# Windowed attention in a mixer block: two tiles per step, the far key as a diagonal, and a reordered first stage

## The chip, the cores and the metric

The kernel runs on one core of a Trainium2 chip. The metric is the device time of one execution in microseconds (us); the median of three runs is 2248.58 us, from 2247.2 to 2249.55.

## What is computed

A decoder block on 2048 rows of 1024 channels, in float32. A conditioning vector gives shift, scale and gate (`c @ w_ada + b_ada`); h is the RMS-normed x, scaled and shifted. One input projection of h gives queries, keys and values of 24 heads in three groups, and the inputs of a pooling mixer and of the gates. A query attends 129 keys of its group, itself and 128 back, in steps of 1, 4 or 16 rows; the third group is done on subsequences of step 8, where the bias leaves every second key out:

```python
def dilated_window_attention(q, k, v, dil, n_back, bias_g):
    dist = BLOCK + i - j
    band_ok = (dist >= 0) & (dist <= n_back)
    logits = jnp.einsum('znqhd,znkhd->znhqk', qb, kb).astype(jnp.float32) * (HEAD_DIM ** -0.5)
    logits = jnp.where(mask[None, :, None], logits + bias[None, None], -jnp.inf)
    p = jnp.exp(logits - m)
    o = jnp.einsum('znhqk,znkhd->znqhd', p.astype(vb.dtype), vb).astype(jnp.float32)
```

The three groups of a head slot are combined with softmax weights of their log denominators, gated, and projected; the pooling branch likewise; the sum goes through `w_out`, the gate, the residual and a final RMS norm.

## The kernel before, in words

The rows are done in two halves of 1024 (`h`). Float32 products are made of three: every operand is split into a high and a low part (`whi`, `wlo`; `hhi`, `hlo`; `khi`, `klo`), and high by high, high by low and low by high are added up. Weights come as 176 raw blocks of 128 x 1024 (`fetch_raw`, line 203, two buffers), and each half block is split by a cast on DVE (`whi`, line 216) and a subtraction on POOL (`wlo`, line 217), as `fetch_part` is called from `tick`.

**First stage** (`first_unit`). x is normed and transposed into `xT`; the conditioning weights come in four blocks of 256 columns (`ada_load`); DVE sums each over 8 chunks (`ada_sum`, lines 377 and 379), PE adds up over partitions (`ada_columns`, line 388), DVE makes scale and shift (lines 391 to 394), ACT makes two chunks of h per block (`h_chunk`, lines 398 and 400) and DVE or POOL their low part (line 401). The k, q and v products of the first unit (line 466) take a chunk as it comes. At its end come the bias tables (`bias_tables`, line 320), built in DRAM from `fd`, and the bias of the first unit (`load_bias`, line 528).

**Units and attention.** A unit is 128 columns of q, k and v of one group: two heads (24 units over both halves). Its main products (`mm3`, line 252) are woven with the attention of the unit before it: `weave` spreads the attention's steps over the 24 steps of the main products. The order on PE and SP, DVE, ACT and POOL is the order in which the code is run through. An attention has 8 tiles of 128 queries. Step s makes the logits of tile s (line 619: for each of the two heads three products of a 64-row operand, in one PSUM bank per head), adds bias and takes the maximum (line 622), the exponentials (line 626); two steps later the current-key logits are transposed (`transposed`, line 650) and `pT` is made twice, once masked for the previous block's values (line 658) and once plain (line 659); a step later come the outputs (`output`, line 669) with `v` and with `vd`, previous minus current values (line 656). The key at distance 128 shares its place with the one at distance 0, so its weight is taken out by a dot product with the identity (line 637, after the add of line 635) and added to the output with `vd` (line 676). Group 0, whose steps are 13 instead of 11, joins the three groups (lines 693 to 708) and transposes the result (`joined`, line 712).

**Second half's h.** While the last products (`out_half`, line 932, column blocks of 256; `yt`, line 946, and the squares on ACT, line 912) of the first half run, `next_h` loads x in pairs of tiles (`new_x`, line 273), norms them (`x_norm`, lines 290, 277 and 292) and transposes (line 336) them chunk by chunk into the new h. Large tiles share `NBIG` = 34 buffers of 128 x 1024, handed out in the order of the code; a load waits until the tile that had the buffer has been read.

## Time and profile before

| | |
|---|---|
| median of three runs | 2248.58 us (2247.2 to 2249.55) |
| the profiled execution, its own time | 2248.75 us |
| its span in the profile | 2246.9 us |
| mean granted clock of TensorE | 0.986 |
| PE busy | 2165.3 us, 11786 products |
| DVE, ACT, POOL busy | 1026.7, 601.8, 762.5 us |

The span is the time from the first to the last instruction in the profile; the execution's own time has 1.85 us more around it. A line of PE rows gives a product of the 128 x 128 array; x2 is two of them in a row, and the time beside it is from the start of the first to the end of the last, so that the distance to the next row's start is what they cost where they follow closely.

### The profile page before, as it was taken

To read this page: it belongs to the slowest core of one execution; us is meant where nothing else is said; L and a number is where in the kernel's file an instruction comes from. 1 tells how busy PE (TensorE), PEld (TensorE's weight loads), DVE (VectorE), ACT (ScalarE), POOL (GpSimd) and SP (SyncE) were. 2 spreads that over 40 slices of the span, in tenths; PEclk is the share of its full clock that TensorE was granted. 3 is DMA by queue.
4 is the path that set the end of the run, shared out by engine and by line. 5 is a ranking of instruction groups with operands and counts; after the bars stand their busy time and mean duration, and the time that the engine had idled before them with its cause. 6 is when DMAs were issued, how large, how long until landed. Compare 5 with 4: busy or idle time off the path is not lost.

```text
span 2246.9 us, 32404 instructions
## 1 busy us (share of the span) xinstructions
PE 2165.3 (96%) x11786; PEld 1810.7 (81%) x11786; DVE 1026.7 (46%) x3188; ACT 601.8 (27%) x1554; POOL 762.5 (34%) x682
## 2 busy tenths in 40 slices
PE   3799999999999999999899999999999999999998
PEld 2588888888887888888888888888888788888898
DVE  5545526355284111115764475664744931111164
ACT  4333323333232001002433333333333320010023
POOL 3322212112134224446752222222222342253375
PEclk7999999999999999999999999999999999999999
DMA  7343312223211112114432322223233111121144
GB/s 275 101 147 105 88 58 83 80 79 88 63 60 47 47 53 88 48 47 160 160 119 74 113 79 88 77 88 93 72 95 91 56 41 53 38 94 47 48 132 160
DMA packets 142687, 198.58 MB, mean 88 GB/s; under 512 B 13542, under 2 KB 109983, under 8 KB 142528
## 3 DMA queue, kind: packets, MB, share of 16 engines
q1 hardware_dynamic: 142528, 196.51, 27.4%
q8 instruction: 94, 1.54, 0.3%
q14 instruction: 65, 0.53, 0.1%
HBM read 157.62 MB, written 35.16 MB: 86 GB/s over the span
## 4 chain that ended last, share of the span: by engine, by line
PE 85%; POOL 4%; DVE 4%; DMA 3%; issue 3%; SPq 1%; ACT 0%; POOLq 0%; DVEq 0%; ACTq 0%
PE mm L252 68%; PE knot L669 6%; PE qk L619 4%; PE mm L932 2%; PE knot L650 2%; POOL wlo L217 2%; DMA wraw<-in_wpk_dram 1%; PE knot L584 1%; DMA wada<-in_w_ada_dram 1%; POOL y L911 1%; PE hp L855 0%; DVE whi L216 0%; PE mm L466 0%; POOL hlo L401 0%; SPq L320 0%
## 5 line engine op out<-in xcount | busy, mean ns | idle before, releaser
L217 POOL TENSOR_TENSOR wlo<-wraw,whi 128x512 fp32r<-128x512 f32 x352 | 468.0, 1333 | 990.3 <-DVE whi L216 536.3
L252 PE MATMUL mm<-hhi,whi 128*128 128x512 f32 x2000 | 649.1, 406 | 2.0 <-DVE klo L508 2.0
L252 PE MATMUL mm<-hlo,whi 128*128 128x512 f32 x2000 | 621.8, 392 | 0.0
L252 PE MATMUL mm<-hhi,wlo 128*128 128x512 f32 x2000 | 619.2, 391 | 0.0
L216 DVE CAST whi<-wraw 128x512 fp32r<-128x512 f32 x352 | 191.8, 549 | 693.3 <-PE mm L252 515.3
L252 PEld LDWEIGHTS mm<-hlo,whi 128*128 128x128 f32 x2000 | 376.7, 188 | 83.2
L252 PEld LDWEIGHTS mm<-hhi,wlo 128*128 128x128 f32 x2000 | 376.3, 188 | 82.9
L252 PEld LDWEIGHTS mm<-hhi,whi 128*128 128x128 f32 x2000 | 355.2, 189 | 79.1 <-issue 2.9
L626 ACT ACTIVATE l<-l,row 128x256 f32<-128x256 f32 (+1 forms) x384 | 181.4, 473 | 253.0 <-DVE row L622 246.4
L749 ACT ACTIVATE sg<-mm 128x1024 f32<-128x1024 f32 x48 | 49.4, 1028 | 554.8 <-PE mm L252 422.5
L622 DVE CUSTOM_DVE_ANT_0 l<-qk,bias 128x256 f32<-128x256 f32 (+1 forms) x384 | 132.8, 383 | 92.0 <-PE qk L619 66.1
L659 ACT COPY pT<-knot 128x256 f32<-128x256 f32 x192 | 71.7, 373 | 329.0 <-DVE pT L658 234.4
L932 PE MATMUL mm<-whi,mhi 128*128 128x256 f32 x512 | 149.8, 293 | 6.0 <-DVE yt L946 3.5
L932 PE MATMUL mm<-whi,mlo 128*128 128x256 f32 x512 | 146.9, 287 | 2.7 <-POOL mlo L756 2.7
L932 PE MATMUL mm<-wlo,mhi 128*128 128x256 f32 x512 | 146.6, 286 | 0.0
L669 PE MATMUL knot<-v,pT 128*128 128x64 f32 x768 | 130.0, 262 | 1.3 <-ACT pT L659 1.3
L656 POOL TENSOR_TENSOR vd<-v 128x128 f32<-128x128 f32 x88 | 52.6, 601 | 224.4 <-DVE row L676 144.7
L669 PEld LDWEIGHTS knot<-v,pT 128*128 128x128 f32 x768 | 113.6, 191 | 4.1 <-ACT pT L659 2.3
L669 PE MATMUL knot<-vd,pT 128*128 128x64 f32 x560 | 108.3, 275 | 0.0
L658 DVE TENSOR_TENSOR pT<-knot,prevm 128x256 f32<-128x256 f32 x140 | 58.9, 420 | 103.1 <-PE knot L669 99.6
L932 PEld LDWEIGHTS mm<-whi,mhi 128*128 128x128 f32 x512 | 100.1, 195 | 6.9 <-DVE yt L946 3.7
L932 PEld LDWEIGHTS mm<-whi,mlo 128*128 128x128 f32 x512 | 99.9, 195 | 3.5 <-POOL mlo L756 3.5
(168 smaller groups left out, 2627.0 us busy)
## 6 DMA issues: line engine op xcount, KB each, us to landing
wraw<-in_wpk_dram SPq DMA_DIRECT2D x176, 512.0 KB, 3.7
rows<-row SPq DMA_DIRECT2D x128, 66.0 KB, 1.6
row<-rows SPq DMA_DIRECT2D x64, 132.0 KB, 3.5
x<-in_x_dram SPq DMA_DIRECT2D x16, 512.0 KB, 4.8
wada<-in_w_ada_dram SPq DMA_DIRECT2D x32, 256.0 KB, 5.5
y<-in_x_dram SPq DMA_DIRECT2D x16, 512.0 KB, 7.5
out_dram<-yo SPq DMA_DIRECT2D x16, 512.0 KB, 6.5
khist<-kh SPq DMA_DIRECT2D x52, 128.0 KB, 2.6
```

Of the source, the lines that this page charges most:

```text
L216: copy(out=hi, in_=raw)
L217: nc.gpsimd.tensor_tensor(out=lo, in0=raw, in1=hi.bitcast(F32), op=ALU.subtract)
L252: nc.tensor.matmul(ps[:, n * 512:(n + 1) * 512], lhsT=w, rhs=m[:, n * 512:(n + 1) * 512], start=(k == 0 and j == 0), stop=(k == nk - 1 and ...
L619: nc.tensor.matmul(qks[i][:, :nk], lhsT=qt[qi][a], rhs=keys[ki][a], start=(j == 0), stop=(j == 2))
L622: nc.vector.tensor_tensor_reduce(out=l[:, i, :nk], in0=qks[i][:, :nk], in1=bt[:, i, 256 - nk:], scale=-1.0, scalar=1e38, op0=ALU.add, op1= ...
L626: nc.scalar.activation(out=l[:, i, :nk], in_=l[:, i, :nk], func=AF.Exp, scale=-1.0, bias=nm[:, i:i + 1], accum_out=rw[:, 130 + i:131 + i])
L656: nc.gpsimd.tensor_tensor(out=vd, in0=d["prev"], in1=vcur[t], op=ALU.subtract)
L658: nc.vector.tensor_tensor(out=pT[:, 0], in0=pps, in1=m, op=ALU.mult)
L659: nc.scalar.copy(out=pT[:, 1], in_=pps)
L669: nc.tensor.matmul(ops[:, hs], lhsT=d["pT"][:, b, i, :], rhs=vv[:, hs], start=(b == 1), stop=(b == 0 or not full))
L749: nc.scalar.activation(out=s, in_=ps, func=AF.Sigmoid)
L932: nc.tensor.matmul(pst[:, pos:pos + 256], lhsT=st, rhs=mv, start=(fresh and i == 0), stop=(last and i == 2))
```

## The change

- **Pairs.** An attention has 4 pair steps instead of 8 tile steps: 7 steps in place of 11, and 8 in place of 13. A step makes the logits of two tiles, 12 products in a run, into one bank per head (the tiles' halves side by side), four transposes into one bank, and the outputs of both tiles, 16 products at most. The tiles `l` (2 buffers instead of 3, of twice the size), `pT` (1 instead of 2) and `vd` (1 instead of 2) hold a pair.
- **Far key.** POOL multiplies the previous-key part of the exponentials by the identity in place; DVE adds that diagonal to the masked `pT`. The dot products (line 637) and the scaled adds (line 676) go. The output copies (line 679) go from DVE to ACT.
- **First stage.** All three raw blocks are asked for at once, the third in a large tile; the even parts are cast ahead of the first scale, the odd ones on ACT behind the first chunk of h; the sums of a block are made in one go; `hlo` of all chunks but the first and the last on POOL; the products of a chunk go by kind (high by high for k, q and v, and so on). The first group's bias table and the bias are asked for right behind the first scale.
- **Buffers.** 33 large tiles instead of 34; small scratch tiles (`junk`, `hraw`, `fs`, the last `yt`) use the buffers of `khist`.

The core of the diff:

```diff
-NBIG = 34
+NBIG = 33
...
-            t = wp.tile([P, HALF], F32, name="wraw", tag="wraw", bufs=2)
+            t = b4(name="wraw") if i == 2 else wp.tile([P, HALF], F32, name="wraw", tag="wraw", bufs=2)
...
-    def fetch_part(copy=nc.vector.tensor_copy):
-
-        i = state["part"]
+    def fetch_part(i=None, copy=nc.vector.tensor_copy):
+
+        if i is None:
+            i = state["part"]
...
-        state["part"] += 1
+        state["part"] = max(state["part"], i + 1)
         if q == 1:
             del raws[b]
+        if q == 1 and b != 2:
             fetch_raw()
...
-        junk = att.tile([P, D], mybir.dt.bfloat16, name="junk", tag="l", bufs=3)
+        junk = att.tile([P, D], mybir.dt.bfloat16, name="junk", tag="khist", bufs=3)
...
-    def bias_tables():
-
-        for g in GORDER:
+    def bias_tables(gs):
+
+        for g in gs:
...
+        accs = [t[:, i * 512:(i + 1) * 512] for t in (b4(name="ada"), b4(name="ada")) for i in range(2)]
         blocks = [ada_load(0)]
-        fetch_raw()
-        fetch_raw()
+        for _ in range(3):
+            fetch_raw()
         for b in range(1, 4):
             blocks.append(ada_load(b))
-        accs = [b4(name="ada")[:, :512] for _ in range(4)]
...
-        ada_columns(0, accs[0])
-        for _ in range(6):
-            fetch_part()
-        ada_sum(blocks[1], accs[1], range(2))
-        wts = [take("col") for _ in range(3)]
+        ps = ada_columns(0, accs[0])
+        for i in (0, 2, 4):
+            fetch_part(i)
+        ada_scale(0, ps)
+        bias_tables(GORDER[:1])
+        load_bias(g, 0, res)
+        wts = [halves(i, P) for i in (0, 2, 4)]
+        state["used"] += 3
         kp, qp = mm(), mm()
         vp = [ps_qk.tile([P, 512], F32, name="vp", tag="qk") for _ in range(2)]
         dsts = [[kp[:, :512], kp[:, 512:]], [qp[:, :512], qp[:, 512:]], vp]
 
-        def products(k, bs):
+        def products(k, js):
             hhi, hlo = hparts[k]
-            for b in bs:
-                whi, wlo = wts[b][k]
-                for j, (w, m) in enumerate(((whi, hhi), (whi, hlo), (wlo, hhi))):
+            for j in js:
+                for b in range(3):
+                    w, m = (wts[b][k][j == 1], hlo if j == 2 else hhi)
                     for n in range(2):
                         nc.tensor.matmul(dsts[b][n], lhsT=w, rhs=m[:, n * 512:(n + 1) * 512],
                                          start=(k == 0 and j == 0), stop=(k == KC - 1 and j == 2))
 
 
         for b in range(4):
-            h_chunk(2 * b, nc.gpsimd if 0 < b < 3 else nc.vector)
+            h_chunk(2 * b, nc.vector if b == 0 else nc.gpsimd)
+            if b == 0:
+                for i in (1, 3, 5):
+                    fetch_part(i, nc.scalar.copy)
+                for w, q in zip(wts, (1, 3, 5)):
+                    w += halves(q, P)
+            h_chunk(2 * b + 1, nc.gpsimd if b < 3 else nc.vector)
             if b < 3:
-                ada_sum(blocks[b + 1], accs[b + 1], range(4 if b else 2, 8))
-            if b < 2:
-                ada_sum(blocks[b + 2], accs[b + 2], range(4))
-            h_chunk(2 * b + 1, nc.gpsimd if b < 3 else nc.vector)
-            if 0 < b < 3:
-                ada_columns(b + 1, accs[b + 1])
-            products(2 * b, range(2))
-            if b == 0:
-                ada_columns(b + 1, accs[b + 1])
-            products(2 * b, range(2, 3))
+                ada_sum(blocks[b + 1], accs[b + 1], range(8))
+            products(2 * b, range(3))
+            if b < 3:
+                ada_scale(b + 1, ada_columns(b + 1, accs[b + 1]))
...
-        bias_tables()
+        bias_tables(GORDER[1:])
...
-        load_bias(g, 0, res)
...
+        def differences(p):
+
+            d = st[p]
+            if d["prev"]:
+                vd = d["vd"] = att.tile([P, 2, P], F32, name="vd", tag="vd", bufs=1)
+                for a, b, prev in d["prev"]:
+                    nc.gpsimd.tensor_tensor(out=vd.rearrange("p j c -> p (j c)")[:, a * P:b * P], in0=prev,
+                                            in1=v[:, (2 * p + a) * P:(2 * p + b) * P], op=ALU.subtract)
+
...
+            l = att.tile([P, 4, 256], F32, name="l", tag="l", bufs=2)
+            d["l"] = l
+            nks = [size(2 * p), size(2 * p + 1)]
+
+            qks = [ps_qk.tile([P, 512], F32, name="qk", tag="qk") for _ in range(2)]
+            for j, nk in enumerate(nks):
+                t = 2 * p + j
+                k0 = kslot(g, t)
+                if nk == P:
+                    keys = [k[:, k0:k0 + P] for k in ks]
+                elif not edge(t):
+                    keys = [k[:, k0 - P:k0 + P] for k in ks]
+                else:
+                    keys = [kh_t[t][:, i, :] for i in range(2)]
+                qt = [q[:, k0:k0 + P] for q in qs]
+                for n, (qi, ki) in enumerate(((0, 0), (1, 0), (0, 1))):
+                    for i in range(2):
+                        a = slice(64 * i, 64 * i + 64)
+                        nc.tensor.matmul(qks[i][:, j * 256:j * 256 + nk], lhsT=qt[qi][a], rhs=keys[ki][a],
+                                         start=(n == 0), stop=(n == 2))
...
+            prev, cur = l[:, f:, 0:P], l[:, f:, P:256]
+            if g < 2:
+                nc.vector.tensor_tensor(out=cur, in0=cur, in1=prev, op=ALU.add)
+                nc.gpsimd.tensor_tensor(out=prev, in0=prev, in1=ident.unsqueeze(1).broadcast_to([P, 4 - f, P]),
+                                        op=ALU.mult)
...
+        def transposed(p, bank):
+
+
+
+
+            d = st[p]
+            f, l = d["from"], d["l"]
+            for n in range(4):
+                nc.tensor.transpose(bank[:, n * P:(n + 1) * P], l[:, n, P:256], ident)
+            yield
+            pps = bank.rearrange("p (n q) -> p n q", q=P)
+            pT = d["pT"] = att.tile([P, 2, 4, P], F32, name="pT", tag="pT", bufs=1)
+            if f < 4:
+                m = prevm[:, g // 2, :].unsqueeze(1).broadcast_to([P, 4 - f, P])
+                nc.vector.tensor_tensor(out=pT[:, 0, f:], in0=pps[:, f:], in1=m, op=ALU.mult)
                 if g < 2:
-                    d["far"] = sm.tile([P, 2], F32, name="far")
-                    junk = att.tile([P, P], mybir.dt.bfloat16, name="dot", tag="dot", bufs=1)
-                    nc.vector.tensor_tensor(out=cur, in0=cur, in1=prev, op=ALU.add)
-                    for i in range(2):
-                        nc.vector.tensor_tensor_reduce(out=junk, in0=prev[:, i, :], in1=ident, scale=1.0, scalar=0.0,
-                                                       op0=ALU.mult, op1=ALU.add, accum_out=d["far"][:, i:i + 1])
-                else:
-                    for i in range(2):
-                        nc.vector.tensor_tensor(out=cur[:, :, i::2], in0=cur[:, :, i::2], in1=prev[:, :, 1 - i::2],
-                                                op=ALU.add)
-
-        def transposed(t, bank):
-
-            d = st[t]
-            nk = d["nk"]
-            pps = bank[:, :256].rearrange("p (i q) -> p i q", i=2)
-            for i in range(2):
-                nc.tensor.transpose(pps[:, i, :], d["l"][:, i, nk - P:nk], ident)
-            yield
-
-            pT = d["pT"] = att.tile([P, 2, 2, P], F32, name="pT", tag="pT", bufs=2)
-            if nk == 256:
-                vd = d["vd"] = att.tile([P, P], F32, name="vd", tag="vd", bufs=2)
-                nc.gpsimd.tensor_tensor(out=vd, in0=d["prev"], in1=vcur[t], op=ALU.subtract)
-                m = prevm[:, g // 2, :].unsqueeze(1).broadcast_to([P, 2, P])
-                nc.vector.tensor_tensor(out=pT[:, 0], in0=pps, in1=m, op=ALU.mult)
+
+                    nc.vector.tensor_tensor(out=pT[:, 0, f:], in0=pT[:, 0, f:], in1=l[:, f:, 0:P], op=ALU.add)
...
+        for s in range(7 if g else 8):
+            parts_ = []
...
+                if s < 7:
                     parts_.append(output(s - 3, bank))
-                if g == 0 and 5 <= s:
-                    parts_.append(joined(s - 5, bank))
-                for p in parts_:
-                    next(p)
-                if s < 8:
-                    logits(s)
-                for p in parts_:
-                    next(p, None)
-            else:
+                if g == 0 and 4 <= s:
+                    parts_.append(joined(s - 4, bank))
+            for p in parts_:
+                next(p)
+            for p in parts_:
+                next(p, None)
+            if 2 <= s < 6:
+                differences(s - 2)
+                if g == 0:
+                    load_rows(s - 2)
+            if s < 4:
                 logits(s)
+                prefetch(2 * s + 2)
+                prefetch(2 * s + 3)
+            if s < 2:
                 flip(s)
+            if 1 <= s < 5:
+                prefetch_v(s - 1)
...
-                    t = att.tile([P, 256], F32, name="yt", tag="pT", bufs=2)
+                    t = att.tile([P, 256], F32, name="yt", tag="khist", bufs=3)
...
-                n_queue = 11 if g else 13
+                n_queue = 7 if g else 8
```

PE, an attention step of group 1 in the first half (`qk` logits, `knot` the bank of transposes and outputs, `mm` the main products). Before:

```order
L650 MATMUL knot<-ident,l 128x128 x2
L669 MATMUL knot<-v_734,pT 128x64
L669 MATMUL knot<-vd,pT 128x64
L669 MATMUL knot<-v_734,pT 128x64
L669 MATMUL knot<-vd,pT 128x64
L619 MATMUL qk<-khi_715,qhi_719 128x256 x2
L619 MATMUL qk<-khi_715,qlo_720 128x256 x2
L619 MATMUL qk<-klo_716,qhi_719 128x256 x2
L252 MATMUL mm<-hhi_516,whi 128x512 x2
```

and a step of the change that has logits, of group 0:

```order
L684 MATMUL knot<-ident,l 128x128 x4
L705 MATMUL knot<-v_4004,pT 128x64 x3
L705 MATMUL knot<-vd,pT 128x64
L705 MATMUL knot<-v_4004,pT 128x64
L705 MATMUL knot<-vd,pT 128x64
L649 MATMUL qk<-khi_3750,qhi_3899 128x256 x2
L649 MATMUL qk<-khi_3750,qlo_3900 128x256 x2
L649 MATMUL qk<-klo_3751,qhi_3899 128x256 x2
L649 MATMUL qk<-khi_3750,qhi_3899 128x256 x2
L649 MATMUL qk<-khi_3750,qlo_3900 128x256 x2
L649 MATMUL qk<-klo_3751,qhi_3899 128x256 x2
L255 MATMUL mm<-hhi_580,whi 128x512 x2
```

The logits of two tiles now stand in one run, and between two steps of the change lie nine pairs of main products where six lay before.

SP, the queue of the loads, at the end of the first stage (`fd` and `btab` the bias tables, `wraw` raw blocks, `cw` and `pm` constants). Before:

```order
L314 DMA fd<-fs_340 8x383
L314 DMA fd<-fs_345 8x383
L314 DMA fd<-fs_350 8x383
L203 DMA wraw<-in_wpk_dram 128x1024 x6
L320 DMA btab<-fd 1024x1x256 x3
L491 DMA cw<-in_cntw_dram 128x64
L528 DMA bias<-btab 128x2x256
```

and in the change:

```order
L317 DMA fd<-fs 8x383 x3
L323 DMA btab<-fd 1024x1x256
L536 DMA bias<-btab 128x2x256
L203 DMA wraw<-in_wpk_dram 128x1024 x5
L323 DMA btab<-fd 1024x1x256 x2
L500 DMA cw<-in_cntw_dram 128x64
```

The bias moved ahead of five raw blocks, with one table in front of it; the sixth raw block (the third of all) went up to the first two.

SP again, the loads of x for the second half, with what each waits for. Before:

```order
L273 DMA x276_9644<-in_x_dram 128x1024 [waits DMAHW5_49,DMAHW0_49]
L273 DMA x277_9646<-in_x_dram 128x1024 [waits DMAHW1_49,DVE_49,Activation_49]
L203 DMA wraw_9713<-in_wpk_dram 128x1024 [waits DMAHW6_49,Pool_49]
L203 DMA wraw_9826<-in_wpk_dram 128x1024 [waits DMAHW7_49,DMAHW3_49,Pool_49]
L273 DMA x279_9847<-in_x_dram 128x1024 [waits DMAHW4_49,PE_49]
L273 DMA x280_9849<-in_x_dram 128x1024 [waits DVE_49,Activation_49]
```

and in the change:

```order
L276 DMA x272_8846<-in_x_dram 128x1024 [waits DMAHW0_49,DVE_49,Activation_49]
L276 DMA x273_8848<-in_x_dram 128x1024 [waits DMAHW1_49,PE_49]
L203 DMA wraw_8915<-in_wpk_dram 128x1024 [waits DMAHW6_49,Pool_49]
L203 DMA wraw_9028<-in_wpk_dram 128x1024 [waits DMAHW7_49,DMAHW3_49,Pool_49]
L276 DMA x275_9049<-in_x_dram 128x1024 [waits DMAHW4_49,DVE_49,Activation_49]
L276 DMA x276_9051<-in_x_dram 128x1024 [waits DMAHW5_49,PE_49]
```

The second tile of each pair now waits for PE (`PE_49`): its buffer was that of a tile of x whose last transposes stand just ahead of the pass that needs the new one.

## Rows read from the trace of the kernel before

**Rows 1.** The page: busy time, and PE's busy tenths in 40 slices.

```profile
PE 2165.3 (96%) x11786; PEld 1810.7 (81%) x11786; DVE 1026.7 (46%) x3188; ACT 601.8 (27%) x1554; POOL 762.5 (34%) x682
...
PE   3799999999999999999899999999999999999998
```

**Rows 2.** Waits of PE: engine, line, waited for; us in total, times, longest.

```profile
PE mm L466 <- DVE hlo L401: 17.4, 1, 17.4
PE qk L619 <- DVE row L622: 12.8, 1, 12.8
...
PE hp L336 <- DVE x L292: 5.6, 4, 3.2
...
PE mm L932 <- DVE yt L946: 3.5, 1, 3.5
```

**Rows 3.** Timeline, first stage: start, length, engine, line; idle before and its releaser.

```profile
27.25 0.15 DVE L394 TENSOR_TENSOR shift_c<-knot,col 128x2 f32<-128x2 f32 x1
...
41.36 0.76 DVE L216 CAST whi<-wraw 128x512 fp32r<-128x512 f32 x2 [10.47 <-DMA wraw<-in_wpk_dram]
...
52.99 0.48 DVE L377 TENSOR_SCALAR ada<-wada,col 128x512 f32<-128x512 f32 x1
...
56.01 0.15 DVE L394 TENSOR_TENSOR shift_c<-knot,col 128x2 f32<-128x2 f32 x1
...
58.61 5.36 POOL L401 TENSOR_TENSOR hlo<-xT,hhi 128x1024 fp32r<-128x1024 f32 x2 [11.22 <-ACT hhi L400]
...
59.10 2.61 DVE L377 TENSOR_SCALAR ada<-wada,col 128x512 f32<-128x512 f32 x1
...
66.27 0.15 DVE L394 TENSOR_TENSOR shift_c<-knot,col 128x2 f32<-128x2 f32 x1
...
71.69 4.40 DVE L216 CAST whi<-wraw 128x512 fp32r<-128x512 f32 x3
...
89.87 0.70 PE L252 MATMUL mm<-hhi,whi 128*128 128x512 f32 x2 [1.99 <-DVE klo L508]
```

**Rows 4.** Timeline, the first logits after the first stage.

```profile
111.81 0.29 DVE L622 CUSTOM_DVE_ANT_0 l<-qk,bias 128x128 f32<-128x128 f32 x1 [16.14 <-DMA bias<-btab]
```

**Rows 5.** Timeline of PE, one attention step between main products.

```profile
279.90 0.39 PE L669 MATMUL knot<-v,pT 128*128 128x64 f32 x2
280.12 0.39 PE L669 MATMUL knot<-vd,pT 128*128 128x64 f32 x2
280.44 0.38 PE L619 MATMUL qk<-khi,qhi 64*128 64x256 f32 x2
280.66 0.28 PE L619 MATMUL qk<-khi,qlo 64*128 64x256 f32 x2
280.78 0.28 PE L619 MATMUL qk<-klo,qhi 64*128 64x256 f32 x2
280.99 0.73 PE L252 MATMUL mm<-hhi,whi 128*128 128x512 f32 x2
281.56 0.63 PE L252 MATMUL mm<-hlo,whi 128*128 128x512 f32 x2
282.03 0.62 PE L252 MATMUL mm<-hhi,wlo 128*128 128x512 f32 x2
```

**Rows 6.** Groups by line: count | busy, mean ns of one | idle before.

```profile
L217 POOL TENSOR_TENSOR wlo<-wraw,whi 128x512 fp32r<-128x512 f32 x352 | 468.0, 1333 | 990.3 <-DVE whi L216 536.3 <-PE mm L252 331.6 <-PE knot L712 37.3
...
L635 DVE TENSOR_TENSOR l<-l 128x256 f32<-128x256 f32 x108 | 60.9, 564 | 10.0 <-ACT l L626 10.0
```

**Rows 7.** Second half's x: timeline, and the page's DMA issues (us to landing last).

```profile
1114.87 0.38 PE L336 MATMUL knot<-ident,x 128*128 128x128 f32 x2
...
1116.86 1.06 ACT L290 ACTIVATE junk<-x 128x1024 bf16<-128x1024 f32 x1 [0.48 <-POOL hlo L344]
...
1121.27 0.48 PE L336 MATMUL hp<-ident,x 128*128 128x128 f32 x1 [0.94 <-DVE x L292]
...
x<-in_x_dram SPq DMA_DIRECT2D x16, 512.0 KB, 4.8
```

More of the change, by code (lines that the diff above doesn't have):

```diff
@@ L550, in attention @@
         edge = lambda t: g == 2 or (g == 1 and t < 4) or (g == 0 and t == 0)
-        st = [{} for _ in range(8)]
+        size = lambda t: P if h == 0 and edge(t) else 256
+        kh_t = {}
+        st = [{} for _ in range(4)]
         if g == 0:
@@ new lines, in prefetch_v @@
+        def prefetch_v(p):
+            d = st[p]
+            d["prev"] = []
+            t = 2 * p
+            ends = [edge(t), edge(t + 1)]
+            if h == 1 and ends[0]:
+                n = sum(ends)
+                vt = att.tile([P, 2, P], F32, name="vhist", tag="vhist", bufs=2)
+                for j in range(n):
+                    ht = {0: 0, 1: (t + j) % 4, 2: t + j}[g]
+                    nc.sync.dma_start(out=vt[:, j, :], in_=vh[g][hp][ht])
+                d["prev"].append((0, n, vt.rearrange("p j c -> p (j c)")[:, :n * P]))
+            a = sum(ends)
+            if a < 2:
+                t0 = t + a - (1, 4)[g]
+                d["prev"].append((a, 2, v[:, t0 * P:(t0 + 2 - a) * P]))
@@ new lines, in differences, with load_rows @@
+        def differences(p):
[5 more added lines that the diff above has]
+                                            in1=v[:, (2 * p + a) * P:(2 * p + b) * P], op=ALU.subtract)
+        def load_rows(p):
+            r3 = st[p]["row3"] = sm.tile([P, 2, 3, RW], F32, name="row3", tag="row3", bufs=3)
+            for j in range(2):
+                t = 2 * p + j
+                nc.sync.dma_start(out=r3[:, j, 0:2, :], in_=rows[h][hp][t * P:(t + 1) * P])
@@ L661, in output @@
[L661 to L673 removed]
+                    nc.vector.tensor_tensor(out=cur[:, :, i::2], in0=cur[:, :, i::2], in1=prev[:, :, 1 - i::2],
+                                            op=ALU.add)
@@ L674, in output @@
+        def output(p, bank):
+            d = st[p]
+            ops = bank[:, :256].rearrange("p (j c) -> p j c", c=P)
+            for j in range(2):
+                full = 2 * j >= d["from"]
+                vs = [(1, vcur[2 * p + j])] + ([(0, d["vd"][:, j, :])] if full else [])
                 for i in range(2):
                     hs = slice(i * 64, (i + 1) * 64)
-                    nc.vector.scalar_tensor_tensor(out=rw[:, hs], in0=d["vd"][:, hs], scalar=d["far"][:, i:i + 1],
-                                                   in1=ops[:, hs], op0=ALU.mult, op1=ALU.add)
-            else:
-                nc.vector.tensor_copy(out=rw[:, 0:P], in_=ops)
+                    for b, vv in vs:
+                        nc.tensor.matmul(ops[:, j, hs], lhsT=d["pT"][:, b, 2 * j + i, :], rhs=vv[:, hs],
+                                         start=(b == 1), stop=(b == 0 or not full))
+            yield
@@ L680, in output @@
             if g:
[L681 to L693 removed]
+                row = d["row"]
@@ new lines, in output @@
+                nc.scalar.copy(out=row[:, :, 0:P], in_=ops)
+                n, r = divmod(2 * p, STEP[g])
+                w = HALF // (2, 1)[g - 1]
+                for j in range(2):
+                    store(rows[h][hp][n * w + r + j:(n + 1) * w:STEP[g], g - 1, :], row[:, j, :], 2)
+                return
+            r3 = d["row3"]
+            nc.scalar.copy(out=r3[:, :, 2, 0:P], in_=ops)
+            nc.vector.tensor_copy(out=r3[:, :, 2, P:], in_=d["nd"])
+            yield
+            nm, den = r3[:, :, :, 128:130], r3[:, :, :, 130:132]
```

160 lines of the change are left out of this document (56 added, 104 removed).

## Prediction

> **What bounds the kernel now.** I read the page first, then the waits of PE, then the timeline of the stretches where PE stands still, and last one attention step row by row. PE is busy 96% of the span, and the row of tenths shows one hole: slices 1, 2 (about 112 us) and little after [rows 1]. So two things can shorten the kernel: less PE time inside the dense stretches, and fewer holes at the start. The list of waits gives the holes: 17.4 us in the first stage for `hlo` (line 401), 12.8 us for the first tile's logits (line 622), 5.6 us where the second half's x is normalised (line 292) and 3.5 us for `yt` next to it (line 946) [rows 2]. No other engine's share comes near; DVE and POOL count only where PE is seen waiting for them.
>
> **Attention in pairs (term A).** No product is dropped or added on PE: the pair step does the same transposes, logit and output products. What changes is how often PE goes in and out of the logit products, which use half of the rows (64*128), and in and out of the step. In the step at 279.90 two output pairs follow each other by 0.22 (0.11 each); the last two before the logits take 0.32, so entering costs 0.10. The first logit pair takes 0.22 to the next, the second 0.12: another 0.10. The third takes 0.21 to the first main product: 0.09 for leaving. That is 0.29 us per group of logits [rows 5]. The main products restart with 0.57 for the first two where two take 0.47 in steady flow (282.03 less 281.56): 0.10, and going over to the transposes costs a little as well, so 0.12 per step [rows 5]. Counts from the code: 24 attentions of 8 tiles are 192 groups now and 96 after; steps are 16 x 11 + 8 x 13 = 280 now and 16 x 7 + 8 x 8 = 176 after. 96 x 0.28 = 27 and 104 x 0.12 = 12 make **A = -39**. Bounds: if PE pays entry and exit for each tile inside the merged group, only the steps remain, -13; if nothing at all is paid for the second tile, -42. I take -39, since the six logit pairs now stand in one run in the order, with nothing of another shape between.
>
> The Trainium skill ("TensorEngine Tiling (Array Packing)", Key Properties) says that changing the tiling mode drains the engine while changing only the tile does not. By that rule the second tile inside a run is free and the sum stays at its -39 here, against -13 for the first rival below. The rows agree as far as one tile goes: its second and third pair pay nothing.
>
> **Far key, copies, buffers.** The 216 dot reductions and 216 scaled adds leave DVE; 56 multiplies by the identity come to POOL and 56 adds to DVE; the row copies go from DVE to ACT. On PE this is worth nothing, because PE does not wait for these engines in the attention stretches [rows 2]. The cover of the new chain: a pair's transposes come two steps after its logits. A pair step is about 7.4 us on PE (nine main pairs at 0.47, six logit pairs at 0.12, 4 transposes and 16 outputs at 0.11) [rows 5], so there are some 15 us in which the exponentials, the add (0.56 for 256 columns, so 1.1 for 512) and the POOL multiply must pass; the multiply has 512 columns like `wlo`, 1.33, and can stand behind one `wlo`, another 1.33 [rows 6]. That is under 5 us with the exponentials aside. After the transposes a second add must be done before the outputs one step later, 7.4 us. Both are covered two- to fourfold. Cost 0; if the cover is gone, see the third rival.
>
> **First stage (term B).** Now the third raw block is asked for behind all of the conditioning weights and the cast waits 10.47 us for it; then DVE does sums and `hlo` late, and PE's long wait follows [rows 2, 3]. The sums come in rounds: scale 0 is ready at 27.3, the next at 56.0, 66.3 and, just ahead of the casts, 71.7 [rows 3]. After the change the third block comes with the other two and only three casts and one `hlo` stand between scale 0 and the sums of round 1, so that these start at about 33.5 (27.3, three casts at 0.4 to 1.5 each, one `hlo` at the 2.7 of POOL's). Eight sums took about 10 us with a POOL `hlo` beside them (56.0 to 66.3 is a round) [rows 3]. Three rounds of 10 to 10.5 put the last scale at 65, 6.5 us earlier. Behind it, three casts of 4.40 stand on DVE now and move behind the last `hlo` [rows 3]; half of that, 2.2, shows at the end, because the last `hlo` is then followed by PE's own products. So the stage's products end some 9 us earlier. Now the main products resume at 89.87, 1.99 after the wait for `klo` began; after, the products of k, q and v end together, so the `klo` wait grows by 1 to 1.5. **-8** for this part. Bounds: 0 if the sums beside POOL stay the chain and run slower, since POOL has two more `hlo`; -18 if only PE's products (72 pairs at 0.47, 34 us from a start at 36) bind.
>
> A row shows that risk: the first sum operation took 0.48 alone and 2.61 beside POOL's `hlo` of 5.36 for two [rows 3]. The Trainium skill ("SBUF — State Buffer", Who interferes with whom) says that DVE and GpSimd share a port pair under an exclusive lock; by that rule each `hlo` moved to POOL stops the sums for its length, and this row agrees. My rounds of 10 us already hold two such meetings. By the rule alone, the two `hlo` that are new on POOL cost the sums 5.4 more, and the time would be 2202.
>
> The bias: it now lands behind three table transfers and a constant, DVE starts at 111.81 after 16.14 of waiting, and PE loses 12.8 us [rows 2, 4]. After, only the table of the first group and the bias go out right after scale 0, some 50 us before their use. The three raw blocks, sums and table have time to land. **-13.** Bounds -9, if the bias comes 4 us late in the new place, and -15, if the pairs right after the pause, which run slow, are counted. The queue SP: the five later raw blocks stand behind this bias load, which waits for the table; that is a few us in a stretch where the next raw block is cast only after 71 us [rows 3]. B = -21, bounds -9 to -33.
>
> **One buffer less (term C).** With 33 buffers the second x tile of a pair in the second half takes the slot of a tile whose last transposes are those just before the pass that needs it; the order shows a wait for PE in place of DVE and ACT. Now: last transposes 1114.87, the next ones due at about 1116.7, and waits of 3.2 and 0.94 [rows 2, 7] because of normalising. After: load from 1115.2, landing 4.8 (the median), to 1120; square, its sum, root and multiply took from 1116.86 to 1121.27, 4.4 us; so PE goes on at 1124.4, 7.7 instead of 4.2 late: +3.5. The second pass of the kind (the other 1.5 of the 5.6) becomes 7.7 as well, +6.2, of which some 2 of the 3.5 come back that PE waits for `yt` right after it [rows 2]. **C = +8.** Bounds: +3 (only the first, and the second wholly hidden) and +20 (each slips by one more round of four squares, which stand ahead of the x square on ACT).
>
> **Sum.** -39 - 21 + 8 = -52 on the profiled execution's 2248.75, which is within 0.2 of the median 2248.58: **2197 us**.
>
> **Rivals.**
> 1. *The group drains between its two tiles.* For: each tile has other query columns and, at the edges, other keys from another buffer. Against: the pairs of one tile already follow each other at 0.12 with weights changing each time [rows 5]. Then A = -13: 2223 us.
> 2. *The start is bound by PE alone*, and the sums are never late. For: PE has only 34 us of products there. Against: the rounds of 10 us [rows 3]. B = -32, the rest as above: 2186 us.
> 3. *Slower: the diagonal's chain is late.* POOL's multiply sits in POOL's order behind `wlo` casts that wait for DVE, and `pT` has one buffer: outputs then wait each pair step for DVE's second add. It decides from the point at which the chain needs more than the 7.4 us between transposes and outputs. Price: 56 pairs with a far key; at one `wlo` of 1.33 each [rows 6], +75, so 2197 + 75 = 2272 us. Against: the two- to fourfold cover above, and DVE has less work than before.
> 4. *It doesn't do what it says*: PE's cost of entering is bound to the logits' own reading and not to changes of shape, so that twelve in a run cost as much per pair, and x at its upper bound takes what the start gives: -13 - 13 + 20 = -6, about 2243 us, a gain that the measurement hardly tells.
>
> **Chances.** Forecast (2184 to 2212) 0.60; first rival 0.15; second 0.14; third 0.06; fourth 0.05. The measurement can tell about 0.2%, 4.5 us, from no change. Faster by more than that: 0.91 (forecast, first two rivals and part of the fourth); within: 0.03; slower: 0.06. The range that leaves out the third, the fourth, and the outer half of the second goes from 2180 to 2226.
>
> **What would show it.** In the changed kernel's profile: logit pairs at 0.12 through all six, with one entry and one exit per step (A right); 0.2 again at the fourth pair (rival 1). No PE wait for `row` near 100 us, and main products resuming near 82 (B); at 90 or later B is wrong. Two PE waits for x of 7 to 8 us near 1065 to 1090 (C). A wait of the outputs for `pT`, many times, would be rival 3. The prediction is wrong if the attention rows show PE time that the step counts don't explain, or if the span outside of the first 120 us and of the x loads falls by less than 13 us.

## The result, and the profile after

The changed kernel takes **2225.2 us** (median of four runs, 2220.3 to 2228.4); the kernel before, on the same chip, 2248.7. The ratio is 0.9894, 95% interval 0.9874 to 0.9915: 1.1% faster, 23.5 us. The forecast was 2197 us, 52 us faster, with a range of 2180 to 2226. The measured time lies inside the range, at its slow end. The sign was right; not half of the gain came. The profiled execution is the shortest of the four, 2220.3 us, so the traces differ by 28.5 us.

The page of the changed kernel, beside [rows 1]:

```profile
PE 2138.4 (96%) x11786; PEld 1809.8 (82%) x11786; DVE 932.8 (42%) x2132; ACT 601.1 (27%) x1493; POOL 819.9 (37%) x675
...
PE   5999999999999999999799999999999999999998
```

PE does the same 11786 products. DVE has a third fewer instructions, POOL 57 us more work, and the hole in slice 2 is gone, but slice 20 went from 8 to 7 tenths, which is the second half's x. The starts of the first main products and of the first products of `out_half` (lines 252 and 932 before, 255 and 970 after) cut both executions into stretches; the last one goes to the start of its last product:

| stretch | before | after | difference |
|---|---|---|---|
| start to first main product | 89.87 | 84.21 | -5.7 |
| units of the first half | 944.61 | 925.61 | -19.0 |
| `out_half`, x of the second half | 120.33 | 124.49 | +4.2 |
| units of the second half | 989.11 | 981.54 | -7.6 |
| second `out_half` | 94.80 | 94.18 | -0.6 |

The first half lost its wait for the bias. In run 9 below, which has the first stage alone, these units take 932.1 us, 12.5 less than before. So of 26.6 us gained in the units, the pairs brought only some 14. Where the rest went is in the list of PE's waits after the change:

```profile
PE knot L744 <- DVE row L740: 17.0, 11, 2.3
PE hp L339 <- DVE x L295: 16.3, 3, 8.0
PE hp L357 <- DVE x L295: 12.4, 4, 9.4
PE knot L391 <- DVE ada L382: 7.9, 3, 6.4
PE mm L475 <- ACT hhi L406: 4.1, 1, 4.1
PE knot L705 <- ACT pT L694: 2.9, 1, 2.9
```

In the first row PE waits 17.0 us in 11 places for the last addition of the join (line 740) before it can transpose the joined result of group 0. The list before has a small row for the same transposes (line 712), which [rows 2] leave out, and the timeline before shows what it is:

```profile
PE knot L712 <- issue: 5.6, 2, 2.9
...
678.73 0.28 DVE L708 TENSOR_TENSOR row<-row 128x128 f32<-128x128 f32 x1
679.11 0.30 PE L712 MATMUL knot<-ident,row 128*128 128x128 f32 x1 [2.70 <-issue]
```

The list names no engine ("issue"), but PE goes on 0.10 us after the end of the join's last addition (line 708), here and at the other place (1788.55). So the join was late twice before the change, for 5.6 us, and eleven times after it. The second row of the list after answers to the third row of [rows 2]: 5.6 us became 16.3.

**A step of the pairs.** The timeline of PE, one step of the change (four transposes and twelve logit products, no outputs yet):

```profile
192.45 0.62 PE L255 MATMUL mm<-hhi,wlo 128*128 128x512 f32 x2
192.91 0.60 PE L684 MATMUL knot<-ident,l 128*128 128x128 f32 x4
193.44 0.39 PE L649 MATMUL qk<-khi,qhi 64*128 64x256 f32 x2
193.66 0.28 PE L649 MATMUL qk<-khi,qlo 64*128 64x256 f32 x2
193.78 0.28 PE L649 MATMUL qk<-klo,qhi 64*128 64x256 f32 x2
193.90 0.28 PE L649 MATMUL qk<-khi,qhi 64*128 64x256 f32 x2
194.02 0.28 PE L649 MATMUL qk<-khi,qlo 64*128 64x256 f32 x2
194.14 0.28 PE L649 MATMUL qk<-klo,qhi 64*128 64x256 f32 x2
194.35 0.73 PE L255 MATMUL mm<-hhi,whi 128*128 128x512 f32 x2
```

The fourth pair, the first of the second tile, follows at 0.12 like those before it; entry (0.22) and exit (0.21) are paid once. That is term A as forecast, on PE's side.

**A join.** The timeline of all engines around one of the eleven waits:

```profile
208.22 1.34 POOL L669 TENSOR_TENSOR l<-l,ident 128x512 f32<-128x512 f32 x1 [6.89 <-DVE l L668]
...
209.53 1.60 POOL L218 TENSOR_TENSOR wlo<-wraw,whi 128x512 fp32r<-128x512 f32 x1
...
209.91 1.78 DVE L693 TENSOR_TENSOR pT<-pT,l 128x512 f32<-128x512 f32 x1
...
211.16 0.33 SPq L203 DMA_DIRECT2D wraw<-in_wpk_dram  x1
...
211.60 0.84 SPq L606 DMA_DIRECT2D row<-rows  x2
211.61 1.09 DVE L737 TENSOR_TENSOR row<-row,e 128x384 f32<-128x384 f32 x1
...
213.82 0.41 DVE L740 TENSOR_TENSOR row<-row 128x256 f32<-128x256 f32 x1
...
215.63 0.17 DVE L723 TENSOR_REDUCE mn<-row 128x4 f32<-128x12 f32 x1 [1.40 <-DMA row<-rows]
215.72 0.41 DVE L740 TENSOR_TENSOR row<-row 128x256 f32<-128x256 f32 x1
...
216.19 0.44 PE L744 MATMUL knot<-ident,row 128*128 128x128 f32 x2 [1.84 <-DVE row L740]
...
218.27 0.68 DVE L693 TENSOR_TENSOR pT<-pT,l 128x512 f32<-128x512 f32 x1
```

Read it from POOL down. The new multiply (line 669) holds `wlo` by 1.34 us. `wlo` frees the raw block buffer, so the next raw block goes out on SP at 211.16, right behind its end; the rows of the other two groups stand behind it on SP and go out at 211.60, one step before they are used. On DVE the reduction of the next pair (line 723) waits for them, and it stands between the two additions of the pair that PE is waiting for. Meanwhile DVE's new addition (line 693) took 1.78 beside POOL's `wlo` and takes 0.68 at 218.27.

### The profile page after: what moved, and what is told of

The parts are those of the page before. It is cut to its first block, busy times and chain, and to the rows that moved or that the text cites. A ratio compares the mean times of both kernels' runs of the same rounds, so it can differ in the third digit from the quotient of the medians.

```text
span 2218.2 us, 30829 instructions
## 1 busy us (share of the span) xinstructions
PE 2138.4 (96%) x11786; PEld 1809.8 (82%) x11786; DVE 932.8 (42%) x2132; ACT 601.1 (27%) x1493; POOL 819.9 (37%) x675
## 4 chain that ended last, share of the span: by engine, by line
PE 39%; DVE 4%; POOL 2%; DMA 2%; issue 2%; ACT 1%; SPq 0%; POOLq 0%; DVEq 0%; ACTq 0%
PE mm L255 32%; PE knot L705 3%; PE qk L649 2%; POOL wlo L218 1%; PE mm L970 1%; DMA row<-rows 1%; DMA wraw<-in_wpk_dram 1%; PE knot L684 1%; PE knot L613 1%; ACT l L659 1%; POOL y L949 1%; DVE wd L729 0%; DVE whi L217 0%; DVE l L668 0%; PE hp L893 0%
## 5 line engine op out<-in xcount | busy, mean ns | idle before, releaser
L218 POOL TENSOR_TENSOR wlo<-wraw,whi 128x512 fp32r<-128x512 f32 x352 | 475.0, 1353 | 991.1 <-DVE whi L217 548.9
L255 PE MATMUL mm<-hhi,whi 128*128 128x512 f32 x2000 | 638.4, 400 | 2.8 <-DVE klo L516 2.8
L255 PEld LDWEIGHTS mm<-hhi,whi 128*128 128x128 f32 x2000 | 364.9, 190 | 75.3 <-issue 3.6
L653 DVE CUSTOM_DVE_ANT_0 l<-qk,bias 128x256 f32<-128x256 f32 (+1 forms) x384 | 126.0, 384 | 122.8 <-PE qk L649 99.4
L659 ACT ACTIVATE l<-l,row 128x256 f32<-128x256 f32 (+1 forms) x256 | 117.0, 458 | 152.4 <-DVE row L653 130.0
L669 POOL TENSOR_TENSOR l<-l,ident 128x512 f32<-128x512 f32 (+1 forms) x56 | 71.6, 1278 | 108.8 <-DVE l L668 98.0
L970 PEld LDWEIGHTS mm<-wlo,mhi 128*128 128x128 f32 x512 | 99.7, 195 | 0.1
L694 ACT COPY pT<-knot 128x512 f32<-128x512 f32 x96 | 56.4, 588 | 156.1 <-DVE pT L690 68.0
```

The lines of the kernel that those rows point to most:

```text
L218: nc.gpsimd.tensor_tensor(out=lo, in0=raw, in1=hi.bitcast(F32), op=ALU.subtract)
L255: nc.tensor.matmul(ps[:, n * 512:(n + 1) * 512], lhsT=w, rhs=m[:, n * 512:(n + 1) * 512], start=(k == 0 and j == 0), stop=(k == nk - 1 and ...
L653: nc.vector.tensor_tensor_reduce(out=l[:, 2 * j + i, 256 - nk:], in0=qks[i][:, j * 256:j * 256 + nk], in1=bt[:, i, 256 - nk:], scale=-1.0, ...
L659: nc.scalar.activation(out=ll, in_=ll, func=AF.Exp, scale=-1.0, bias=nd[:, j, i:i + 1], accum_out=nd[:, j, 2 + i:3 + i])
L669: nc.gpsimd.tensor_tensor(out=prev, in0=prev, in1=ident.unsqueeze(1).broadcast_to([P, 4 - f, P]), op=ALU.mult)
L694: nc.scalar.copy(out=pT[:, 1], in_=pps)
```

## The experiments

The changed kernel was run again beside the first of these; its median there, 2227.5, is what they are held against. Later runs were on other chips; the kernel before took 2248.2 to 2249.3 us on all of them.

**1. The changed kernel again.** 

> The changed kernel itself, beside which the next three are read. In its profile the execution took 2220.3 us, its other runs 2223.5 to 2228.4. Both theories: median near 2225, with PE waiting 15 to 25 us in all for the join of group 0 (line 744, for the last addition on DVE, line 740).

2227.5 us (2223.3 to 2232.1), ratio to before 0.990 (0.989 to 0.992). The profiled execution took 2232.06, 11.8 more than the first one, and PE's waits for line 740 were 23.0 us in 12 places instead of 17.0 in 11. So 6.0 of the 11.8 us lie in this wait. The mean granted clock was 0.983 instead of 0.987, so that products were slower too.

**2. The rows one step earlier.**

```diff
-                if g == 0:
-                    load_rows(s - 2)
...
             if 1 <= s < 5:
                 prefetch_v(s - 1)
+                if g == 0:
+                    load_rows(s - 1)
```

> The rows of the other two groups (row<-rows) are asked for one pair step earlier, in the same three buffers. Theory 1 (late rows): the join waits because these rows are asked for one step before their use, behind a raw block load on SP, and a reduction that waits for them stands on DVE ahead of the previous pair's last addition. Then the 17 us of waits for line 740 nearly vanish, 12 to 20 us faster than the changed kernel, near 2208. Theory 2 (far key): the join waits because POOL and DVE carry the diagonal; then the time stays within 4 us of the changed kernel.

2207.0 us (2206.0 to 2208.5): 20.5 us faster than the changed kernel, and the spread is gone. Theory 1's number came, with 6.6 us of the wait left:

```profile
PE knot L744 <- DVE row L740: 6.6, 6, 2.4
```

**3. No diagonal.** Lines 669 and 693 are taken out.

> Leaves out the far key's separation: no multiply by the identity on POOL, no addition to the masked pT on DVE, so the key at distance 128 takes the wrong value row. Theory 2: the join's waits vanish, 12 to 20 us faster. Theory 1: the rows come earlier only by the 1.3 us that the multiply holds up the raw block in front of them, so that the waits shrink by at most half: 0 to 10 us faster.

2198.4 us, 29 us faster: more than either theory gave, and far more than theory 1 allows. In its trace DVE waits as long as ever for the rows, yet it costs PE little. The waits of PE, and DVE's timeline at the same join:

```profile
PE knot L739 <- DVE row L735: 5.9, 3, 3.2
```

```profile
211.02 0.88 DVE L735 TENSOR_TENSOR row<-row 128x256 f32<-128x256 f32 x2
211.82 1.22 DVE L530 SCALAR_TENSOR_TENSOR qlo<-mm,qhi 128x1024 fp32r<-128x1024 f32 x1
214.96 0.17 DVE L718 TENSOR_REDUCE mn<-row 128x4 f32<-128x12 f32 x1 [1.93 <-DMA row<-rows]
```

Without the diagonal both additions are done at 211.9, before the reduction waits. So neither theory holds alone: late rows and far key both count. Not all of the gain is accounted for: between the profiled executions of runs 1 and 3 lie 34.1 us, of which 17.1 are the join's wait and 4.2 waits of the outputs; the mean granted clock rose from 0.983 to 0.989.

**4. The logits parted again.** In a step, transposes, outputs and flips go between the two tiles' logits.

```diff
-        def logits(p):
+        def logits(p, between):
...
                         nc.tensor.matmul(qks[i][:, j * 256:j * 256 + nk], lhsT=qt[qi][a], rhs=keys[ki][a],
                                          start=(n == 0), stop=(n == 2))
+                if j == 0:
+                    between()
...
```

> The two tiles' logits are parted again: transposes, outputs and value flips of the step stand between them, so PE goes in and out of the half-row products twice a step, 96 times more in all. If the entry and exit are what the pairs save (theory A, 0.29 to 0.35 us each): 28 to 34 us slower than the changed kernel. If the saving comes from fewer steps or from elsewhere: within 6 us.

2243.2 us (2239.8 to 2248.6): 15.7 us slower, between the two. PE's rows give the full price:

```profile
196.52 0.61 PE L255 MATMUL mm<-hhi,wlo 128*128 128x512 f32 x2
197.06 0.38 PE L649 MATMUL qk<-khi,qhi 64*128 64x256 f32 x2
197.29 0.28 PE L649 MATMUL qk<-khi,qlo 64*128 64x256 f32 x2
197.40 0.28 PE L649 MATMUL qk<-klo,qhi 64*128 64x256 f32 x2
197.61 0.66 PE L686 MATMUL knot<-ident,l 128*128 128x128 f32 x4
198.20 0.38 PE L649 MATMUL qk<-khi,qhi 64*128 64x256 f32 x2
...
198.74 0.74 PE L255 MATMUL mm<-hhi,whi 128*128 128x512 f32 x2
```

From the last main pair to the next it is 2.22 us where the changed kernel's step above took 1.90: 0.32 for one more entry and exit, 31 us for 96. Half of it did not reach the end: the wait for the join's last addition (line 742 in this run) fell from 23.0 to 12.7 us, which fits longer steps that give DVE more time; that is 10 of the 15 us. That a slower PE step pays part of itself back is a first sign that the join is short of time.

**5 and 9. The first stage alone.** The kernel before with the raw block, first stage and bias edits, attention as before. In the first of the two the old `load_bias` at the end of the stage was left in by mistake.

> The kernel before with the first stage, bias and raw block changes alone; attention by single tiles and 34 buffers as before. If the terms add up as the change's profile reads (main products resume 4 to 6 us earlier, no wait for the bias): 18 to 22 us faster than before, near 2229. If the earlier start is taken up by a later wait: within 8 us of before.

2238.4 us, 10.5 below before: PE still waits 6.3 us for the first logits (12.8 before, as the table in front of this load is already there).

> As the run with the first stage alone (2238.4), whose edit had left the bias load at its old place as well, so that the first logits still waited for it: now the old load is gone. If the bias's own place is what the rest of term B rests on: the wait of 6.3 us and the slow products behind it go, 7 to 9 us below that run, near 2230. If not: the same 2238.

2230.0 us against 2249.3, ratio 0.9914 (0.9901 to 0.9928): the wait is gone, 8.4 us more. Term B is worth **19.2 us** by itself, against 21 in the sum.

**6. x apart.** Three of the four late x tiles in tiles that are idle then.

```diff
-                tiles += [new_x(1, p + 4), new_x(1, p + 5)]
+                x5 = att.tile([P, D], F32, name="x", tag="l", bufs=2)
+                x4 = b4(name="x") if p == 0 else att.tile([P, D], F32, name="x", tag="pT", bufs=1)
+                load_x(1, p + 4, x4)
+                load_x(1, p + 5, x5)
+                tiles += [x4, x5]
```

> The changed kernel with three of the four late x tiles in the idle tiles of the logits and pT, so that no load of x waits for PE. If term C was right in kind: PE's waits for the normalised x (line 295) in the second half fall from 16 us to about 6, and the time is 4 to 8 us below the changed kernel's 2227.5. If the load was not what ends them: no change.

2214.9 us, 12.6 below the changed kernel's 2227.5. PE's waits for x:

```profile
PE hp L339 <- DVE x L295: 5.7, 4, 3.2
```

In its trace the stretch of `out_half` takes 117.2 us instead of the changed kernel's 124.5: 7.3 us, inside what was expected. The rest of the 12.6 can't be put down to x: the join's wait was 16.8 us here, as in the first trace of the change (17.0; 23.0 in run 1), and against that trace's 2220.3 us the profiled execution here, 2215.3, is 5.0 faster. Run 14 below repeats the comparison without the join's wait.

**7. The multiply on DVE.** `nc.gpsimd` becomes `nc.vector` in line 669.

> The changed kernel with the multiply by the identity on DVE instead of POOL; the same result. If POOL's multiply matters because it holds up wlo, the raw block and so the rows behind it on SP: the join's waits shrink, 6 to 15 us faster than the changed kernel. If it is DVE that is short of time: no gain, or up to 10 us slower.

2208.3 us, 19.2 faster. DVE has more to do and PE waits less, 13.0 us in 9 places: it was not DVE's own load that counted, but the multiply's place on POOL. DVE's wait for the rows (line 723) fell from 16.6 us in run 1 to 8.6, as expected if POOL holds up the raw block; what DVE's operations lose beside POOL goes too, and the run does not part the two.

**10. The rows on ACT's queue.** `nc.sync.dma_start` becomes `nc.scalar.dma_start` in `load_rows`, same step.

> The changed kernel with the loads of the two other groups' rows issued by ACT's queue in the same step, no longer behind the raw block on SP. If the raw block in front of them is what makes them late: the reduction on DVE no longer waits for them, the join's waits fall by more than half, 10 to 20 us faster than the changed kernel. If asking one step before the use is too late in itself: less than 5 us faster.

2216.6 us, 10.9 faster. DVE no longer waits for the rows at all, but PE still waits 15.0 us for line 740, now in 15 places, eight of them of 0.45 to 0.63 us. At the join shown above, where PE waited 1.84 us, it waits 0.49 (in run 2 it does not wait there). So rows in time take away a part of the wait and not all of it; why more is left here than in run 2, where it was 6.6 us, is not shown.

**11 and 12. DVE in the order of the code** (`et.DVE` added to the engines in manual order after the first stage; in both kernels only PE and SP are held to the order of the code there), once with the change as it is and once with the edits of run 8.

> The changed kernel with DVE too in the order of the code after the first stage, so that both additions of a pair stand ahead of the next pair's reduction; rows and far key untouched. If the rows' lateness costs PE time because the waiting reduction stands between the two additions: the join's waits for the last addition fall from 17 to 23 us to under 8, and the time by 8 to 20 us, unless other waits come from the new order elsewhere. If the additions are late of themselves: the join's waits stay above 12 us.

2256.2 us: 28.7 slower instead of faster, with 45.1 us of waits for line 740. Both additions now stand ahead of the next reduction, but the rest of DVE's order changed with it: the code has the join's arithmetic behind the logits of the same step. At 208.76 the reduction (line 723) starts right behind the addition of those logits (line 668), the last addition ends at 213.34, and PE waits 2.93 us. So this order is no cure. What the reduction's place between the additions costs by itself, the run does not show; in the timeline above the second addition stood behind 1.40 us of the reduction's waiting, of the 1.84 that PE waited.

> Rows early, multiply on DVE, x apart (2194.4 us together) and DVE in the order of the code. What was left of the join's waits was 6.5 us: if the order ends these, 2186 to 2192; if the order costs elsewhere, above 2195.

2244.9 us, with 42.0 us of waits for the join.

**13. The join a step later.**

```diff
-        for s in range(7 if g else 8):
+        for s in range(7 if g else 9):
...
-                if g == 0 and 4 <= s:
-                    parts_.append(joined(s - 4, bank))
+                if g == 0 and 5 <= s:
+                    parts_.append(joined(s - 5, bank))
...
-                n_queue = 7 if g else 8
+                n_queue = 7 if g else 9
```

> The changed kernel with the join of group 0 one step later (nine steps instead of eight), so that two steps lie between a pair's outputs and its transposes as in the kernel before; rows, far key and DVE's order as the change has them. If the join waits because one pair step is too short for what DVE has to do and wait for in it: the waits of PE for the last addition fall from 17 to 23 us to under 5, and the time by 15 to 25 us, less a few tenths for each of the eight steps that are added. If the lateness is passed on from pair to pair: the waits stay above 12 us.

2208.2 us (2206.7 to 2210.5), 19.3 faster. The list of PE's waits has no line 744 any more:

```profile
PE hp L339 <- DVE x L295: 16.3, 3, 8.0
PE hp L357 <- DVE x L295: 12.3, 4, 9.3
PE knot L391 <- DVE ada L382: 8.0, 3, 5.6
PE knot L705 <- ACT pT L694: 7.5, 6, 2.8
```

The rows, POOL's multiply and DVE's order are all as the change has them. So the cause of the wait is the one step in which all of this has to fit; each of runs 2, 3, 7 and 10 took something out of that step. A smaller wait has come up, of the outputs for `pT` (7.5 us; 2.9 in the changed kernel).

**14 and 15. The later join with x apart, and with the multiply on DVE as well.**

> The join a step later and three of the four late x tiles apart. The two waits have nothing to do with each other: 9 to 12 us below the run with the later join alone.

2202.7 us, 5.5 below run 13 and not 9 to 12. PE's waits for x fell from 16.3 to 6.7, and the stretch of `out_half` took 117.3 us. Most of the 7.3 us that the stretch shows reach the end.

> As the last, with the multiply by the identity on DVE. If the later join has covered what the far key cost: within 4 us of the last. If DVE or POOL still holds the join: 5 us or more faster.

2195.9 us (2192.6 to 2196.0), 6.8 below run 14; the waits for `pT` on ACT fell from 7.6 to 3.4 us. POOL's multiply costs something beside the join too.

**8. The best version.** Rows one step earlier, the multiply on DVE and x apart, together:

> Rows one pair step earlier, the multiply on DVE and the x tiles apart, together. If the three causes are separate: 2227.5 less 20.5 for the rows, less 4 to 8 for x, less a few us of what is left of the join's waits: 2194 to 2203. If they overlap or DVE becomes late: above 2204.

**2194.4 us** (2194.0 to 2195.3), ratio to before 0.9758 (0.9745 to 0.9771): 2.4% faster than before and 33 us below the changed kernel. PE's wait for the join is 6.5 us in 4 places. Run 15 reaches the same within its spread. The gains overlap: 20.5 (rows) and 19.2 (multiply) and 5 to 7 (x) would be 45 and more if they added up, since the first two shorten the same wait.

## Why the forecast was wrong, point by point

**Term A, the pairs on PE: right in mechanism, 6 us too large.** Adding up what all steps take beyond the main products' own pace, waits left out (the median of each kind of step times its count), gives 351 us before and 318 after: -33 against -39. The units of runs 9 and 8, which both still have some 6 us of join waits, agree: 1921.2 and 1889.2 us, 32 apart. A merged group of logits saves more than I put, since the step's restart belongs to it: in full steps 1.82 twice became 3.28, 0.36 per pair. But the 0.12 for each step that goes was counted for all 104; steps without logits save nothing (1.12 twice against 2.23), because transposes, outputs and main products follow each other without a gap. The first rival (draining between the tiles) is out by the 0.12 at the fourth pair, and run 4 shows the price that merging saves. That the measured 2225 comes so near this rival's 2223 is chance. The Trainium skill ("TensorEngine Tiling (Array Packing)", Key Properties) says that a change of the tiling mode drains the engine and a change of the tile alone does not; a tile there is a part of the array and not 128 queries. The rows of both kernels agree: 0.12 from pair to pair while the half-row shape stays, also where the next 128 queries begin, and 0.2 where the shape changes, at entry and exit.

**Term B: right.** 21 forecast, 19.2 measured alone. Inside it, -8 for the stage was -5.7. The rounds of sums ended at 45.48, 57.06 and 68.63:

```profile
28.65 0.15 DVE L400 TENSOR_TENSOR shift_c<-knot,col 128x2 f32<-128x2 f32 x1
...
45.48 0.15 DVE L400 TENSOR_TENSOR shift_c<-knot,col 128x2 f32<-128x2 f32 x1
...
57.06 0.15 DVE L400 TENSOR_TENSOR shift_c<-knot,col 128x2 f32<-128x2 f32 x1
...
59.65 5.38 POOL L407 TENSOR_TENSOR hlo<-xT,hhi 128x1024 fp32r<-128x1024 f32 x2 [6.18 <-ACT hhi L406]
...
68.63 0.15 DVE L400 TENSOR_TENSOR shift_c<-knot,col 128x2 f32<-128x2 f32 x1
```

A round is 11.6 us with two `hlo` of POOL beside it, not 10 to 10.5; the last scale comes at 68.6, not 65. That is 3.6 us later, 1.4 of it because scale 0 comes at 28.65; the rule that the prediction cites would have added 5.4 for the two new `hlo`. The main products resume at 84.21 here and at 83.9 to 87.2 in the other runs that have this first stage. The second rival, a start bound by PE alone, is out.

**Term C: right in kind, +8 forecast, +4.2 in the stretch.** The two waits of 7.7 that I put are 7.95 and 5.11 us:

```profile
1101.92 0.47 PE L339 MATMUL hp<-ident,x 128*128 128x128 f32 x1 [7.95 <-DVE x L295]
1122.25 0.48 PE L339 MATMUL hp<-ident,x 128*128 128x128 f32 x1 [5.11 <-DVE x L295]
```

More came back than 2 us: the 3.5 us wait for `yt` of [rows 2] is gone from the list. Taking the loads apart gave 7.3 us in the stretch, and 5.5 in the whole time where the join no longer waits (run 14).

**The step that failed: "Cost 0" for far key, copies and buffers.** I followed the new chain from the logits to the outputs, found it covered two- to fourfold, and stopped there. The ground, that PE does not wait for these engines in the attention stretches, was not right either: the join's two waits before, 5.6 us, stand in the list that I read, put down to no engine. Group 0's results go on: rows of the other groups are loaded, DVE joins the three and PE transposes the result. In single tiles this had two steps between outputs and join, and the rows were asked for three steps ahead of their use; in pairs it has one step, and the rows are asked for one step ahead, with twice the combining work for each pair. The loop's bounds in the diff say both (`joined(s - 4)` against `output(s - 3)`, `load_rows(s - 2)`), and I counted steps without asking what had been waiting in them. In that one step the far key counts after all: POOL's multiply delays `wlo`, the raw block and the rows on SP, and DVE's additions are stretched beside POOL (1.78 against 0.68). The Trainium skill ("SBUF — State Buffer", Who interferes with whom) says that DVE and GpSimd share a port pair under an exclusive lock, and that a DVE instruction with two SBUF inputs contends with a GpSimd instruction that reads SBUF. This trace agrees: the addition (from `pT` and `l`) began 0.38 us after `wlo` (1.60) and took 1.10 longer than alone, so that it ended 0.56 after `wlo` did. I had used that rule for the first stage only, and priced it at 5 us there.

What this wait takes is 17.0 to 23.0 us in the two traces of the change, and 19.3 us by run 13; the 5.6 us that stood in the kernel before are part of it. Without it the changed kernel would stand at 2208, about 41 below before. The remaining 11 to the forecast are not parted by runs; read from the traces, 6 of term A, 2 of term B, some 8 of waits of the outputs for `pT` (9.1 in run 13 against 1.3 before) and the eight added steps stand on one side, and 4 of term C and the 5.6 of the join before on the other. The third rival had the diagonal's chain in view, but at the outputs and as an all or nothing at 75 us; its place, `pT`, shows 2.9 us.

## What to carry to other kernels

When a software pipeline's steps are merged, write down for every later stage how many steps lay between producer and consumer before, and how many lie there now, in time and not in steps: loads that were asked for three steps ahead and consumers that came two steps later are part of the cover. Look up what ends a wait that a list puts down to no engine: before the change it already told that the join was tight. Follow a chain to its last consumer on the bounding engine, and do so for each kind of unit, not only for the commonest. On an in-order queue look at what stands just in front of a small load: here a block load whose buffer was freed by POOL set the time of 132 KB of rows.

## What the runs showed of the hardware that was not expected

Holding DVE to the order of the code cost 28.7 us, though it put both additions of the join ahead of the reduction that waits for rows. The runs show no more of the cause than that the join's arithmetic then starts behind the logits of the same step. And a change between transposes, outputs and main products costs PE nothing (2.23 us for a step of two tiles against twice 1.12), while going into the half-row logits and out again cost 0.32 us in run 4's step.
